# Two layers of a hybrid diffusion backbone: the low parts of the differential keys in 128-row tiles with a zero half, and a rotary step in place

## The chip, the core and the metric

The kernel runs on one core of a Trainium2 chip. The core has a matrix engine (TensorE, PE in the rows; its loads of the stationary operand are shown apart as PEld), VectorE (DVE), ScalarE (ACT), GpSimd (POOL) and SyncE (SP), each with its own queue of instructions that it works off in order, and 16 DMA engines. The metric is the device time of one launch in microseconds (us); less is better.

## What is computed

Two layers work on 640 tokens: 128 context tokens (block 0) and 512 latent tokens (blocks 1 to 4). Each layer has three parallel mixers, a gated merge and a feed-forward part. The change touches one of the mixers, the differential attention. It has 4 heads; each has two queries and two keys of 64 channels, and one value of 128:

```python
def _diff_attention(q, k, v, lam, lam_init):
    s = jnp.einsum('bqhcd,bkhcd->bhcqk', q, k).astype(jnp.float32) * DIFF_HD ** -0.5
    p = jax.nn.softmax(s, axis=-1)
    a = p[:, :, 0] - lam * p[:, :, 1]
    o = jnp.einsum('bhqk,bkhe->bqhe', a.astype(v.dtype), v)
    return (_head_rmsnorm(o) * (1.0 - lam_init)).astype(v.dtype)
```

Latent queries see 640 keys (128 cached ones and the 512 latent ones), context queries see the 128 context keys. Queries and keys of latent tokens are rotated first (`_rope`): x becomes x cos + x' sin, where x' is x with its two halves of 32 channels exchanged and one of them negated.

## The kernel before

All matrix products are made of float32r parts: a value is a high part that the format holds, and the rest as a low part, and a product is the sum of high by high, high by low and low by high. Time is spent mostly in such triples of products (lines 131 to 133 and 1087 to 1089).

The program is written stage by stage: latent attention (`mla`), differential attention (`diff`), retention (`ret`), merge and output projection, feed-forward part; and this twice. A scheduler then sets the order of the instructions on each engine, from the program's order and its own estimate of when each can start. During the attention stages, pieces of other products (gates of line 995 and 996, values of the retention of lines 786 to 789, all with tile G) are handed out by `fill()` between the steps of the attention, one to three pieces a step, so that the matrix engine has work while the softmax runs.

In `diff` each head is built by `build(hd)`, one head ahead of its use: GpSimd issues the DMAs that fetch values (tile V), keys (rk) and queries (rq); `rope` (lines 417 to 429) rotates them with four VectorE operations and two scratch tiles; ScalarE and VectorE make high and low parts; transposes on TensorE (lines 729, 730, 748) bring channels to the partitions, and copies put the result into K1, K2 and Q. For half c of a head (c is 0 or 1), K1 holds in its 128 rows the high part of key c twice. K2 holds the low parts of both: rows 0 to 63 for c = 0, rows 64 to 127 for c = 1. Q holds in 128 rows the high and the low part of query c, the high part where K2 has its rows. So one score takes two products into the same bank, one over 128 rows and one over 64:

```python
pe.matmul(o, Q[:, c, q0:q0 + 128], K1[:, c, k0:k0 + n], start=True, stop=False)
pe.matmul(o, Q[rows, c, q0:q0 + 128], K2[rows, k0:k0 + n], start=False, stop=True)
```

These are lines 807 and 808, with `rows = slice(64 * c, 64 * c + 64)`. For a latent block they come four times (two halves c, two groups of 320 keys), for the context block twice, with 128 keys. Two tiles S of two banks each take the scores in turn.

`diff_head` then runs, for each block in the order 1, 2, 3, 4, 0: the row maximum on VectorE (line 435), the exponential on ScalarE (line 437, into tile dp, four buffers), the weighted difference of the two halves on VectorE (line 821, into tile aw, one buffer), five transposes of aw (line 833), a copy on ScalarE (tile at, two buffers), and five products with V (line 837). The second half, from the transposes on (`diff_av`), is issued one block later than the first. After the last block of a head `diff_end` normalises the head and transposes it (line 851); the tile osb that it reads has one buffer, so the first product with V of the next head waits until those transposes are done.

Of the kernel before, what the change touches and what calls it, by code (L numbers as in the profile page):

```python
# [21 lines left out]
P = 128  # L22
# [3 lines left out]
T = 640  # L26
# [9 lines left out]
NA = 416            # columns of the first product of the latent attention; 256 more follow  # L36
FFN_PARTS = ((0, 8), (8, 16), (16, 22))

# columns of the constant table
C_ID, C_ONE, C_DF, C_DB, C_SEL, C_VEC = 0, 128, 256, 384, 512, 514  # L40
C_C64, C_S64, C_C32, C_S32, C_END = 520, 776, 1032, 1160, 1288
# columns of the per-partition parameter table
V_ADA, V_N1, V_N2, V_FG, V_QN, V_KVN, V_END = 0, 96, 112, 128, 136, 142, 146
# columns of the replicated-row table
# [3 lines left out]
class Kern:  # L48
# [25 lines left out]
    def G(self):  # L74
        """A bank for a product: two in turn, one of them only while attention has the other."""
        self.gi ^= 1
        tag = "G" if self.gi or self.filling else "O"
        return self.ps.tile([P, 512], F32, tag=tag, name="G", bufs=1)
# [11 lines left out]
    def plan(self, points, *gens):  # L90
        """Spread the pieces of (generator, number of pieces[, from, to]) evenly over the next calls of fill()."""
# [25 lines left out]
    def load_w(self, src, cols):  # L117
        """A weight unit [128, cols] from DRAM, as a part that float32r holds and the rest."""
# [8 lines left out]
    def mm3(self, out, steps):  # L127
        """out = sum of lhsT^T rhs over steps of (lhs_hi, lhs_lo, rhs_hi, rhs_lo)."""
# [6 lines left out]
    def rsqrt(self, out, ssq, n, mul, mul2=1.0):  # L135
        """out = mul2 / sqrt(ssq * mul + EPS), for [128, n]."""
# [19 lines left out]
    def setup(self):  # L156
# [12 lines left out]
        # silu of the two conditioning vectors, padded to 32 columns  # L169
# [7 lines left out]
    def rows_setup(self):  # L177
        # log_sigmoid(x) = min(x, 0) - log1p(exp(-|x|)), log1p(e) = 2 atanh(e / (2 + e))
# [38 lines left out]
    def ada_vectors(self, pool):  # L217
        """silu of the two conditioning vectors on every partition."""
# [8 lines left out]
    def ada_rows(self, l, b0, b1, pool):  # L227
        """Modulation with output columns on partitions and the sums on VectorE, a column block a step."""
# [16 lines left out]
    def mod_scale(self, l, which):  # L245
        """A = norm_g * (1 + sc) as [128, 8, 2]; which 0 for the mixers, 1 for the ffn."""
# [10 lines left out]
    def square(self, h, k, x, pool):  # L257
        """Adds the squares of row tile k of a half of x to its sum."""
# [26 lines left out]
    def modulate(self, l, which, h, k, xn, a, ht, pool):  # L285
        """Row tile k of h = xn * A + sh, in float32r parts."""
# [13 lines left out]
    def norm(self, l, which, h, x, a, pool, ps):  # L300
        """h-th half of rmsnorm(x) * A + sh from the sum of squares, in float32r parts (hi, lo) [128, 8, n]."""
# [9 lines left out]
    def start(self):  # L311
        """First norm and first part of the first product, as the columns of the modulation come in."""
# [79 lines left out]
    def tok(self, act, k, b):  # L392
        """(hi, lo) stationary block b of an activation in two halves."""
        h, o = (0, 128 * b) if b < 2 else (1, 128 * b - 256)
        hi, lo = act[h]
        return hi[:, k, o:o + 128], lo[:, k, o:o + 128]

    def a_steps(self, act, b, units):
        """For 128 tokens of block b, act^T W; units: list of (hi, lo, first k, n k) with [128, nk, N]."""
# [17 lines left out]
    def rope(self, pool, out, x, b, nb, nh, hd, tag="avs"):  # L417
        """out = rope(x) for sample blocks b .. b + nb: x [128, nb, nh, hd]."""
# [13 lines left out]
    def softmax(self, sv, p, z, scale, tot=None):  # L432
        """p = exp(scale (sv - max sv)), tot = sum p, z = 1 / tot, for one score row a partition in sv."""
# [7 lines left out]
    def mla(self, l, act, yraw, pool, first=None):  # L441
# [10 lines left out]
        # the k tiles hold two heads each time: rows 0:64 k_nope, rows 64:96 k_pe  # L452
        NK = 3
        kts = [pool.tile([P, 2, TK], F32R, name=f"kt{i}") for i in range(NK)]
        for g in range(2):
# [12 lines left out]
            if g == 0:  # L468
                self.rsqrt(rs[:, 0, :], ss[:, 0, :], NB, 1.0 / 256)
                # decoupled keys  # L470
# [15 lines left out]
                # compressed keys and values  # L486
# [43 lines left out]
        # decoupled queries of all heads, by tokens  # L530
# [81 lines left out]
    def mla_av(self, pool, v, hh, blks, pt, n, y, last=None):  # L612
        """y [64, n] += p^T v over key blocks; pt(kb) gives (hi, lo) [128, n]."""
# [11 lines left out]
    def mla_head(self, pool, qt, q0, kt, v, hh, y, last=None):  # L625
        """Two blocks of sample queries of one head."""
# [55 lines left out]
    def diff(self, l, act, yhi, ylo, ctx):  # L682
# [4 lines left out]
        # lambda  # L687
# [9 lines left out]
        K1, K2, Q, V = {}, {}, {}, {}  # L697
        a6 = "p (a c r) -> p a c r"

        def build(hd):  # L700
# [8 lines left out]
            # keys  # L709
            k1 = K1[hd] = pool.tile([P, 2, TK], F32R, tag="K1", name="K1", bufs=2)  # L710
            k2 = K2[hd] = pool.tile([P, TK], F32R, tag="K2", name="K2", bufs=2)
# [6 lines left out]
            self.rope(pool, rv[:, 2:6], rv[:, 2:6], 0, 4, 2, 64, tag="rp")  # L718
            for j in range(3):
# [13 lines left out]
                d.tensor_copy(k2[:, cs], t2[:, 0:256])  # L733
            # queries, as hi(q1) lo(q1) lo(q2) hi(q2)
# [4 lines left out]
            self.rope(pool, rv[:, 1:5], rv[:, 1:5], 0, 4, 2, 64, tag="rp")  # L739
# [19 lines left out]
    def diff_proj(self, l, act, pool):  # L759
        """Queries, keys, values of the differential attention, by tokens, to DRAM; a generator."""  # L760
# [15 lines left out]
    def ret_values(self, l, act, pool):  # L776
        """Values and doubled silu gates of the retention, by tokens, to DRAM; a generator."""
# [15 lines left out]
    def diff_head(self, pool, Q, K1, K2, V, nlam, lam_init, yhi, ylo):  # L793
# [3 lines left out]
        for b in (1, 2, 3, 4, 0):  # L797
# [4 lines left out]
            for c in range(2):  # L802
                S = self.S()
                rows = slice(64 * c, 64 * c + 64)
                for j in range(2 if b else 1):
                    o, k0, n = (S[:, j, 0:320], 128 + 320 * j, 320) if b else (S[:, 0, 0:128], 0, 128)
                    pe.matmul(o, Q[:, c, q0:q0 + 128], K1[:, c, k0:k0 + n], start=True, stop=False)  # L807
                    pe.matmul(o, Q[rows, c, q0:q0 + 128], K2[rows, k0:k0 + n], start=False, stop=True)  # L808
# [8 lines left out]
            # p0 / t0 - lam p1 / t1 = (p0 - (lam t0 / t1) p1) / t0, the last division after the product with v  # L817
            r = zt[:, 4:5]
            d.scalar_tensor_tensor(r, zs[1][0], nlam, zs[0][1], op0=ALU.mult, op1=ALU.mult)
            aw = pool.tile([P, T], F32, tag="aw", name="aw", bufs=1)  # L820
# [354 lines left out]
    def run(self):  # L1175
# [95 lines left out]
        xctx.close()  # L1271


# [1 line left out]
def consts():  # L1275
    f = np.float32
    i = np.arange(128)
# [117 lines left out]
```

## Time and profile before

| | |
|---|---|
| median of 3 timed runs | 2520.76 us (2518.72 to 2521.29) |
| span of the profiled execution | 2522.9 us |
| TensorE busy in the span | 2471.6 us (98%) |
| VectorE, ScalarE, GpSimd busy | 1500.7, 987.9, 170.8 us |
| differential attention, layer 0 and layer 1 | about 297 to 500 us, and 1535 to 1740 us |

The profiled execution's span is the only time that it has; it is 2.1 us (0.08%) longer than the median of the timed runs. Products on TensorE overlap: the duration that a row gives is that of one product from its start to its modelled end, and the next one may start long before that. What a product costs the engine is therefore read from the distance between two starts in the timeline, not from its duration.

### The profile page before, as it was taken

Reading aid. Unit: us, or ns where it says so; the run is one execution under the profiler, and the core shown is the slowest. Engines: PE = TensorE matmul, PEld = TensorE weight load, DVE = VectorE, ACT = ScalarE, POOL = GpSimd, SP = SyncE. Lnnn points to the kernel's source line nnn. Section 1 sums busy time; section 2 is a strip of 40 time slices with the busy share of each in tenths; the row PEclk is TensorE's granted clock in tenths of the full one; section 3 lists DMA queues with packets and bytes.
Section 4 is the critical chain, followed back from the end, with each engine's and each line's share of the span. In section 5 each row is a group of like instructions: output and inputs, shape, how many; then the busy total and the mean of one; then the engine's idle time right before and its main releaser. Section 6 shows DMA issues by size and latency. Waiting matters only on the chain.

```text
span 2522.9 us, 42747 instructions
## 1 busy us (share of the span) xinstructions
PE 2471.6 (98%) x17236; PEld 2378.8 (94%) x17236; DVE 1500.7 (59%) x3439; ACT 987.9 (39%) x2102; POOL 170.8 (7%) x298
## 2 busy tenths in 40 slices
PE   8999999999999999999999999999999999999997
PEld 5999988899999999999999998889999999999997
DVE  5877665466798676585477866655663562323334
ACT  5656454532324322222376654554222352122123
POOL 0000210010010000010000012001000000000001
PEclk9999999999999999999999999999999999999999
DMA  6212321131553454453231123113222221222221
GB/s 259 76 56 70 101 65 52 64 132 59 186 182 126 142 164 157 139 184 107 65 126 60 52 76 115 62 44 114 79 96 88 72 71 67 84 68 84 67 74 61
DMA packets 70677, 248.94 MB, mean 99 GB/s; under 512 B 9840, under 2 KB 10064, under 8 KB 69584
## 3 DMA queue, kind: packets, MB, share of 16 engines
q1 hardware_dynamic: 46944, 164.12, 19.6%
q0 software_dynamic: 23248, 81.36, 9.8%
q8 instruction: 135, 2.21, 0.4%
q10 hardware_dynamic: 288, 0.73, 0.1%
q14 instruction: 62, 0.51, 0.1%
HBM read 225.97 MB, written 20.22 MB: 98 GB/s over the span
## 4 chain that ended last, share of the span: by engine, by line
PE 91%; issue 3%; DVE 3%; ACT 2%; DMA 1%; POOL 0%; DVEq 0%; ACTq 0%; POOLq 0%
PE G L131 13%; PE G L132 12%; PE G L133 12%; PE S L1089 8%; PE S L1088 8%; PE S L1087 8%; PE S L131 6%; PE S L132 6%; PE S L133 6%; PE S L808 2%; PE S L807 1%; PE Tp L645 1%; PE O L837 1%; PE O L620 1%; PE O L619 1%
## 5 line engine op out<-in xcount | busy, mean ns | idle before, releaser
L112 ACT CAST whi<-raw 128x1024 fp32r<-128x1024 f32 (+4 forms) x298 | 299.2, 1018 | 755.6 <-PE G L132 265.4
L115 DVE TENSOR_TENSOR wlo<-raw,whi 128x1024 fp32r<-128x1024 f32 (+4 forms) x298 | 349.1, 1182 | 358.4 <-ACT whi L112 356.2
L131 PE MATMUL G<-ghi,whi 128*128 128x256 f32 (+1 forms) x704 | 217.2, 309 | 3.1 <-DVE x L1049 3.1
L133 PE MATMUL G<-ghi,wlo 128*128 128x384 f32 (+1 forms) x704 | 216.5, 308 | 0.0
L132 PE MATMUL G<-glo,whi 128*128 128x384 f32 (+1 forms) x704 | 216.4, 308 | 0.0
L1087 PE MATMUL S<-h1hi,whi 128*128 128x384 f32 x640 | 214.0, 334 | 0.0
L1088 PE MATMUL S<-h1lo,whi 128*128 128x384 f32 x640 | 213.9, 334 | 0.0
L1089 PE MATMUL S<-h1hi,wlo 128*128 128x384 f32 x640 | 213.9, 334 | 0.0
L1089 PE MATMUL S<-h0hi,wlo 128*128 128x256 f32 x704 | 199.2, 283 | 1.0 <-DVE wlo L115 0.9
L1088 PE MATMUL S<-h0lo,whi 128*128 128x256 f32 x704 | 198.8, 283 | 0.0
L1087 PE MATMUL S<-h0hi,whi 128*128 128x256 f32 x704 | 198.1, 283 | 0.0
L238 DVE SCALAR_TENSOR_TENSOR junk<-rawr,csr 128x1024 bf16<-128x1024 f32 x160 | 194.9, 1218 | 1.3
L131 PE MATMUL G<-whi,h1hi 128*128 128x256 f32 x624 | 179.3, 288 | 2.7 <-ACT rvs L786 1.0
L133 PE MATMUL G<-whi,h1lo 128*128 128x256 f32 x624 | 177.9, 285 | 0.0
L132 PE MATMUL G<-wlo,h1hi 128*128 128x256 f32 x624 | 177.1, 284 | 0.0
L1049 DVE SCALAR_TENSOR_TENSOR x<-G,mod,x 128x128 f32<-128x128 f32 (+1 forms) x192 | 77.4, 435 | 138.1 <-PE G L133 137.6
L435 DVE TENSOR_REDUCE mx<-S 128x1 f32<-128x640 f32 (+1 forms) x160 | 113.8, 714 | 75.1 <-PE S L808 53.6
L1089 PEld LDWEIGHTS S<-h0hi,wlo 128*128 128x128 f32 x704 | 134.6, 191 | 2.8 <-DVE wlo L115 2.5
L131 PEld LDWEIGHTS G<-ghi,whi 128*128 128x128 f32 x704 | 132.1, 188 | 4.6 <-DVE x L1049 3.3
L1088 PEld LDWEIGHTS S<-h0lo,whi 128*128 128x128 f32 x704 | 134.3, 191 | 0.3
L1087 PEld LDWEIGHTS S<-h0hi,whi 128*128 128x128 f32 x704 | 134.3, 191 | 0.0
L132 PEld LDWEIGHTS G<-glo,whi 128*128 128x128 f32 x704 | 132.1, 188 | 0.2
(428 smaller groups left out, 6908.0 us busy)
## 6 DMA issues: line engine op xcount, KB each, us to landing
raw<-w_ffn_in SPq DMA_DIRECT2D x88, 512.0 KB, 3.6
rawr<-w_adat POOLq DMA_DIRECT2D x80, 512.0 KB, 3.9
raw<-w_gate SPq DMA_DIRECT2D x48, 512.0 KB, 3.3
raw<-w_ffn_out SPq DMA_DIRECT2D x32, 512.0 KB, 3.7
raw<-w_diff SPq DMA_DIRECT2D x24, 512.0 KB, 3.4
raw<-w_branch SPq DMA_DIRECT2D x24, 512.0 KB, 3.7
raw<-w_ret SPq DMA_DIRECT2D x24, 512.0 KB, 3.3
raw<-w_ada SPq DMA_DIRECT2D x16, 512.0 KB, 9.7
```

The source lines that it names most:

```text
L112: (eng or self.act).copy(hi, src)
L115: (eng or self.dve).tensor_tensor(lo, src, hi.bitcast(F32), op=ALU.subtract)
L131: self.pe.matmul(out, lh, rh, start=i == 0, stop=False)
L132: self.pe.matmul(out, lh, rl, start=False, stop=False)
L133: self.pe.matmul(out, ll, rh, start=False, stop=i == n - 1)
L238: self.tc.keep_in_program_order(d.scalar_tensor_tensor(junk, raw, 1.0, self.csr[:, i, :], op0=ALU.mult, op1=ALU.mult, accum_out=mod[:, n, ...
L435: self.dve.tensor_reduce(mx, sv, axis=AX.XY if len(sv.shape) == 3 else AX.X, op=ALU.max)
L808: pe.matmul(o, Q[rows, c, q0:q0 + 128], K2[rows, k0:k0 + n], start=False, stop=True)
L1049: self.dve.scalar_tensor_tensor(x[h][:, n, c0:c1], ps[:, c0:c1], g[:, n, gi:gi + 1], x[h][:, n, c0:c1], op0=ALU.mult, op1=ALU.add)
L1087: self.pe.matmul(o, lh, rh, start=k == 0, stop=False)
L1088: self.pe.matmul(o, lh, rl, start=False, stop=False)
L1089: self.pe.matmul(o, ll, rh, start=False, stop=k == nk - 1)
```

## The change

There are four edits, all in `diff` and what it calls.

1. K2 is no longer one tile with both halves. There are two tiles `K2z`, made once per layer (one for even and one for odd heads), each of 128 rows by 2 halves by 768 keys. For c = 0 rows 64 to 127 are set to zero on GpSimd, for c = 1 rows 0 to 63. The copy of the low parts (line 733 before) becomes two copies of 64 rows each. The second product of a score now takes all 128 rows of Q and of K2z; the zero rows add nothing.
2. `rope_in_place` takes the place of `rope` for the keys and queries of this stage. It has the same four operations, in another order, with one scratch tile of one buffer.
3. `aw` is no tile of its own: the weighted difference overwrites the first of the two tiles dp.
4. Tile `at` has one buffer instead of two.

Comments are removed throughout the file; they are left out here.

```diff
+    def rope_in_place(self, pool, x, b, nb, nh, hd, tag):
...
+        u = pool.tile([P, nb * nh * hd], F32, tag=tag, name="rp", bufs=1).rearrange("p (a h d) -> p a h d", a=nb, h=nh)
+        d = self.dve
+        d.tensor_tensor(u[:, :, :, 0:hh], x[:, :, :, hh:hd], s[:, :, :, 0:hh].to_broadcast([P, nb, nh, hh]), op=ALU.mult)
+        d.tensor_tensor(u[:, :, :, hh:hd], x[:, :, :, 0:hh], s[:, :, :, hh:hd].to_broadcast([P, nb, nh, hh]), op=ALU.mult)
+        d.tensor_tensor(x, x, c, op=ALU.mult)
+        d.tensor_tensor(x, x, u, op=ALU.add)
...
+        k2z = [pool.tile([P, 2, TK], F32R, name=f"K2z{i}") for i in range(2)]
+        for t in k2z:
+            nc.gpsimd.memset(t[64:128, 0, :].bitcast(F32), 0.0)
+            nc.gpsimd.memset(t[0:64, 1, :].bitcast(F32), 0.0)
...
-            k2 = K2[hd] = pool.tile([P, TK], F32R, tag="K2", name="K2", bufs=2)
+            k2 = K2[hd] = k2z[hd % 2]
...
-            self.rope(pool, rv[:, 2:6], rv[:, 2:6], 0, 4, 2, 64, tag="rp")
+            self.rope_in_place(pool, rv[:, 2:6], 0, 4, 2, 64, "rp")
...
-                d.tensor_copy(k2[:, cs], t2[:, 0:256])
+                d.tensor_copy(k2[0:64, 0, cs], t2[0:64, 0:256])
+                d.tensor_copy(k2[64:128, 1, cs], t2[64:128, 0:256])
...
-                rows = slice(64 * c, 64 * c + 64)
...
-                    pe.matmul(o, Q[rows, c, q0:q0 + 128], K2[rows, k0:k0 + n], start=False, stop=True)
+                    pe.matmul(o, Q[:, c, q0:q0 + 128], K2[:, c, k0:k0 + n], start=False, stop=True)
...
-            aw = pool.tile([P, T], F32, tag="aw", name="aw", bufs=1)
+            aw = ps[0]
...
-            at = pool.tile([P, T], F32, tag="at", name="at", bufs=2)
+            at = pool.tile([P, T], F32, tag="at", name="at", bufs=1)
```

The scheduler gives the two stages of `diff` a new order; outside of them the order of every engine stays, and that of SyncE, which issues the weight loads, is the same throughout. The stage holds the same matrix products as before. Three places show what moves. The names with K stand for K1 and K2 of one head, G for a bank that a filled-in product takes, Tp for a bank of transposes.

On TensorE, the scores of the first latent block of the first head in layer 0, first before:

```order
L807 MATMUL S<-K_3873,Q 128x320
L808 MATMUL S<-K_3874,Q 128x320
L729 MATMUL Tp<-identr,kh 128x128 x4
L807 MATMUL S<-K_3873,Q 128x320
L808 MATMUL S<-K_3874,Q 128x320
L807 MATMUL S<-K_3873,Q 128x320
L808 MATMUL S<-K_3874,Q 128x320
L807 MATMUL S<-K_3873,Q 128x320
L808 MATMUL S<-K_3874,Q 128x320
```

and after:

```order
L825 MATMUL S<-K_3879,Q 128x320
L826 MATMUL S<-K2z_3868,Q 128x320
L825 MATMUL S<-K_3879,Q 128x320
L826 MATMUL S<-K2z_3868,Q 128x320
L825 MATMUL S<-K_3879,Q 128x320
L826 MATMUL S<-K2z_3868,Q 128x320
L825 MATMUL S<-K_3879,Q 128x320
L826 MATMUL S<-K2z_3868,Q 128x320
L767 MATMUL Tp<-identr,qs 128x128 x4
L747 MATMUL Tp<-identr,kh 128x128 x4
```

The eight products of the block stay eight and stay in pairs; the transposes that stood among them now stand behind them.

On GpSimd, the start of the stage in layer 0 (V, rk and rq are values, keys and queries that come in by DMA), first before:

```order
L152 DMA ra<-rows 128x256
L704 DMA V<-cdv 128x128
L706 DMA V<-dproj 128x128
L707 DMA V<-dproj 128x4x128
L704 DMA V<-cdv 128x128
L706 DMA V<-dproj 128x128
L707 DMA V<-dproj 128x4x128
L713 DMA rk<-dproj 128x128
```

and after:

```order
L152 DMA ra<-rows 128x256
L714 MEMSET K2z_3868 64x768
L715 MEMSET K2z_3868 64x768
L714 MEMSET K2z_3869 64x768
L715 MEMSET K2z_3869 64x768
L722 DMA V<-cdv 128x128
L724 DMA V<-dproj 128x128
L725 DMA V<-dproj 128x4x128
L722 DMA V<-cdv 128x128
L724 DMA V<-dproj 128x128
L725 DMA V<-dproj 128x4x128
L731 DMA rk<-dproj 128x128
```

The four fills of zeros stand ahead of all fetches of the first two heads.

On VectorE, the key and query parts of the first head in layer 0 (rp is the scratch tile of the rotation, kl and qs hold low parts), first before:

```order
L426 TENSOR_TENSOR rp<-rq,ct 128x512
L427 TENSOR_TENSOR rp<-rq,ct 128x8x32
L428 TENSOR_TENSOR rp<-rq,ct 128x8x32
L733 COPY K_3874<-Tp 128x256
L115 TENSOR_TENSOR kl<-rk,kh 128x256 x2
L429 TENSOR_TENSOR rq<-rp 128x512
L115 TENSOR_TENSOR qs<-rq,qs 128x128
```

and after:

```order
L439 TENSOR_TENSOR rp<-rq,ct 128x8x32
L751 COPY K2z_3868<-Tp 64x256
L752 COPY K2z_3868<-Tp 64x256
L440 TENSOR_TENSOR rp<-rq,ct 128x8x32
L115 TENSOR_TENSOR kl<-rk,kh 128x256 x2
L441 TENSOR_TENSOR rq<-rq,ct 128x512
L115 TENSOR_TENSOR wlo<-raw,whi 128x1024
L442 TENSOR_TENSOR rq<-rq,rp 128x512
```

One copy of the low key part has become two, and the operation over 512 columns of the rotation comes after the two over halves.

## Rows read from the trace of the kernel before

**Rows 1.** Page, part 4: the chain that ended last, by engine.

```profile
PE 91%; issue 3%; DVE 3%; ACT 2%; DMA 1%; POOL 0%; DVEq 0%; ACTq 0%; POOLq 0%
```

**Rows 2.** Lines 807 and 808: duration ns min/median/max, first and last start, forms.

```profile
L807 PE MATMUL S<-K,Q x144: 220/410/417, 316.3 to 1724.2; 128*128 128x320 f32 x128, 128*128 128x128 f32 x16
...
L808 PE MATMUL S<-K,Q x144: 322/410/413, 316.5 to 1724.5; 64*128 64x320 f32 x128, 64*128 64x128 f32 x16
```

**Rows 3.** Timeline of PE, one latent block: start us, duration us, instruction.

```profile
346.81 0.39 PE L807 MATMUL S<-K,Q 128*128 128x320 f32 x1
...
349.51 0.45 PE L131 MATMUL G<-h1hi,whi 128*128 128x384 f32 x1
349.79 0.34 PE L132 MATMUL G<-h1lo,whi 128*128 128x384 f32 x1
349.97 0.33 PE L133 MATMUL G<-h1hi,wlo 128*128 128x384 f32 x1
```

**Rows 4.** Timeline of PEld in the same block; in brackets idle time before.

```profile
347.47 0.19 PEld L807 LDWEIGHTS S<-K,Q 128*128 128x128 f32 x1 [0.15 <-issue]
347.81 0.18 PEld L808 LDWEIGHTS S<-K,Q 64*128 64x128 f32 x1 [0.16 <-issue]
```

**Rows 5.** Timeline of PE, scores of the latent attention (96 rows, 320 columns).

```profile
137.07 0.31 PE L131 MATMUL S<-kt,qt 96*128 96x320 f32 x1
...
137.95 0.31 PE L131 MATMUL S<-kt,qt 96*128 96x320 f32 x1
```

**Rows 6.** Timeline of PEld, the load for the product at 137.07.

```profile
136.93 0.19 PEld L131 LDWEIGHTS S<-kt,qt 96*128 96x128 f32 x1
```

**Rows 7.** Timeline of PE, half a context block (128 columns) of the differential attention.

```profile
354.76 0.22 PE L807 MATMUL S<-K,Q 128*128 128x128 f32 x1
354.91 0.33 PE L808 MATMUL S<-K,Q 64*128 64x128 f32 x1
...
355.44 0.33 PE L131 MATMUL G<-h1hi,whi 128*128 128x384 f32 x1
```

**Rows 8.** Timeline of PE, scores of the latent attention with 128 columns.

```profile
147.76 0.27 PE L132 MATMUL S<-kt,qt 96*128 96x128 f32 x1
147.87 0.27 PE L133 MATMUL S<-kt,qt 96*128 96x128 f32 x1
```

**Rows 9.** Busy time by stretch: us, PE, PEld, DVE, ACT, POOL busy, PEclk, DMA share, GB/s.

```profile
300.00:380.00 80.00, 79.02 (x508) 68.84 (x506) 55.52 (x140) 45.53 (x118) 11.62 (x19) 1.00 0.24 78
...
100.00:140.00 40.00, 39.90 (x317) 39.63 (x317) 30.82 (x73) 23.71 (x55) 3.24 (x6) 1.00 0.23 77
```

**Rows 10.** Waits of DVE, 297 to 500 us: total us, times, longest us.

```profile
DVE mx L435 <- PE S L808: 26.9, 27, 2.2
DVE aw L821 <- PE Tp L833: 13.7, 9, 4.1
```

**Rows 11.** Line 733, columns as in rows 2.

```profile
L733 DVE CAST K<-Tp x24: 411/420/426, 302.9 to 1666.2; 128x256 fp32r<-128x256 f32 x24
```

**Rows 12.** Line 808 from 300 to 380 us, columns as in rows 2.

```profile
L808 PE MATMUL S<-K,Q x30: 323/410/413, 316.5 to 375.8; 64*128 64x320 f32 x28, 64*128 64x128 f32 x2
```

**Rows 13.** Timeline of POOL at the start of the stage in layer 0.

```profile
279.58 0.75 POOL L707 DMA_DIRECT2D V<-dproj  x1
288.45 0.54 POOL L713 DMA_DIRECT2D rk<-dproj  x1 [8.11 <-DVE lpr L690]
```

**Rows 14.** Groups of POOL by line and form: busy us, mean ns, then idle before.

```profile
L1169 POOL TENSOR_TENSOR x<-x,nr 128x384 f32<-128x384 f32 x4 | 4.8, 1234 | 619.0 <-ACT nr L278 619.0
...
L1370 POOL MEMSET const-float32-0.0<- 128x1 f32 x1 | 0.1, 98 | 0.2 <-issue 0.2
```

**Rows 15.** Busy time in a stretch of lower clock, columns as in rows 9.

```profile
429.70:433.10 3.40, 3.40 (x17) 3.40 (x17) 2.46 (x14) 0.58 (x1) 0.00 (x0) 0.50 0.02 5
```

**Rows 16.** Timeline of PE, from the last product with V of head 0 to its end.

```profile
367.94 0.49 PE L837 MATMUL O<-V,at 128*128 128x128 f32 x2
...
386.97 0.76 PE L851 MATMUL Tp<-ct,osb 128*128 128x128 f32 x5
```

More of the change, by code (lines that the diff above doesn't have):

```diff
@@ L429, in rope @@
         d.tensor_tensor(out, t, u, op=ALU.add)
+    def rope_in_place(self, pool, x, b, nb, nh, hd, tag):
+        cc, ss = (C_C64, C_S64) if hd == 64 else (C_C32, C_S32)
+        hh = hd // 2
+        c = self.ct[:, cc + hd * b:cc + hd * (b + nb)].rearrange("p (a d) -> p a d", a=nb).unsqueeze(2).to_broadcast([P, nb, nh, hd])
+        s = self.ct[:, ss + hd * b:ss + hd * (b + nb)].rearrange("p (a d) -> p a d", a=nb).unsqueeze(2)
+        u = pool.tile([P, nb * nh * hd], F32, tag=tag, name="rp", bufs=1).rearrange("p (a h d) -> p a h d", a=nb, h=nh)
[4 more added lines that the diff above has]
+        d.tensor_tensor(x, x, u, op=ALU.add)
     def softmax(self, sv, p, z, scale, tot=None):
@@ L738, in build @@
             rv = r.rearrange("p a (c d) -> p a c d", c=2)
-            self.rope(pool, rv[:, 1:5], rv[:, 1:5], 0, 4, 2, 64, tag="rp")
+            self.rope_in_place(pool, rv[:, 1:5], 0, 4, 2, 64, "rp")
             for b0, nb in ((0, 1), (1, 2), (3, 2)):
```

## The prediction

> **What bounds the kernel now.** I began with the chain of work that ended last: 91% of it is TensorE, and 3% is "issue", time in which an engine stood still although nothing that the profile shows held it [rows 1]. So what shortens TensorE's own work counts nearly in full, as long as nothing else takes its place, and the "issue" share asks for a look of its own. The lines that the change touches come next: 144 products each on lines 807 and 808, of which 128 have 320 columns and 16 have 128, the first over 128 rows, the second over 64 [rows 2].
>
> Their durations say little, since products overlap. The timeline says more. In one latent block the first of eight score products starts at 346.81, the product after them at 349.51 and the next at 349.79, where that kind then goes on at 0.17 to 0.18 us a piece [rows 3]. Eight products in 2.70 us are 0.34 each. The weight loads show where that goes: the load for line 807 starts at 347.47 and the one for line 808 at 347.81, each after 0.15 to 0.16 us in which the load path did nothing [rows 4]. Nothing is loaded ahead.
>
> The reader should hold the scores of the latent attention beside this. They have as many columns and 96 rows, one shape after another, and start every 0.147 us (137.07 to 137.95, six products) [rows 5]; the load for the product at 137.07 begins at 136.93, under the product ahead of it [rows 6]. The same work thus goes at 0.147 where the row shape stays, and at 0.34 where 128 and 64 rows alternate. That the alternation is the cause, and not something else in these pairs, is my reading of the two rows; the change takes away the alternation and nothing else of it.
>
> **The change part by part.** *Second product over 128 rows.* In the block above, first product to the second one after the scores is 2.98 us [rows 3]. At the other pace it would be 8 x 0.147 for the scores and 0.17 for the product at 349.51, 1.35 us. The loss is 1.63. A little of it may stay: transposes stand ahead of the first score, and the first gap may be long for that reason too. I take 0.09 for it, half of what a gap between two shapes costs over one shape (0.34 - 0.147 = 0.19). So 1.54 to 1.63 a block, and with 32 latent blocks (4 blocks, 4 heads, 2 layers) 49 to 52 us. For the context block one pair and its follower take from 354.76 to 355.44, 0.68 us [rows 7], where 128 columns with one shape go at 0.11 [rows 8]: 0.11 + 0.11 + 0.17 = 0.39, so 0.29 lost, and 16 such pairs give 4.6. Together 54 to 57 us. Where a block is cut by other products each cut costs part of a gap, which the new order merely moves. I take 54.
>
> The Trainium skill has a rule that speaks against this term. Its page "TensorE: Matmul & The Clock Gate" (Part 3, The mechanism) says that a weight load overlaps a running product "only when row_grp differs", that is, only when the two use different rows of the array. By that rule products over all rows would keep their loads exposed, the sum of this term would be 0, and the time would stay near 2521. The trace disagrees [rows 5, 6]: products over the same 96 rows have their loads hidden.
>
> *Two copies for one.* Line 733's copy of 128 rows takes 0.42 us, 24 times [rows 11]. I price a 64-row copy of as many columns between half and all of that and take all, since the number of columns is unchanged: 24 more at 0.42 are 10.1 us of VectorE in both layers. VectorE is busy 55.5 of 80 us in the densest stretch [rows 9], and 26.9 us of its idle time in one layer is waiting for scores [rows 10]. That idle time covers it: nothing on the path. If the cover is gone, the price is the 10.1.
>
> *Rotation in place.* The same four operations over the same columns on one engine: nothing. With one scratch buffer the next rotation waits for the last, and both are on VectorE, in order.
>
> *aw inside dp.* VectorE no longer waits for the transposes of the block before to free aw; that is 13.7 us of its waits in layer 0, the longest 4.1 [rows 10]. Behind that wait the maxima of the next block and splits of weights were queued. TensorE was fed meanwhile, so I count no gain; it is slack that the next edit may use. In return one of four dp buffers stays taken until its transposes, and an exponential may wait for it.
>
> *One buffer for at.* ScalarE's copy now waits for the last product with V of the block before. Where only a few products stand between two such groups TensorE could wait. That goes into the allowance below.
>
> *Zeros.* Four fills per layer stand on GpSimd ahead of the fetches of V, keys and queries. This trace has no such fill. From below: a fill of one column takes 0.098 us, so 0.4 for four. From above: an operation with two inputs over 384 columns takes 1.234 [rows 14], so 768 columns 2.5, and 9.9 for four. I lean to the upper half, since the columns count. The first fetch of keys waited 8.11 us on GpSimd anyway, for VectorE [rows 13], so it is late by at most 1.8 us, and the first score comes some 28 us after that fetch (288.45 to 316.3) [rows 2, 13]. I take nothing; 0 to 3.6 in both layers is in the range.
>
> *Less slack.* With TensorE ahead by 1.6 us a block, the softmax has less time. In the densest stretch TensorE is not busy for 0.98 of 80 us [rows 9]. Over the two stages, some 400 us, that is 4.9. I allow as much again. VectorE reaches 77% (30.82 of 40) in the latent attention with TensorE idle for 0.10 us [rows 9], so a high share alone doesn't starve it.
>
> *The clock.* For 3.4 us in this stage the granted clock was 0.50, which is 1.2 in place of 2.4 GHz [rows 15], and 17 products started where twice as many could. If it fell because the pairs had left TensorE thinly used, and doesn't fall any more, about 1.7 us a layer come back, 3.4 in all. I count that in the range only.
>
> The sum: 54 saved, 4.9 given back, 49 net. Against the profiled span of 2522.9 us that is 2474; the timed runs had a median 2.1 lower, so 2472.
>
> **The rivals.** *VectorE becomes the bound.* From 300 to 380 us stand 30 pairs, 28 of them long [rows 12], which shortens the stretch by 28 x 0.386 + 2 x 0.29 = 11.4 to 68.6 us (0.386 is twice 0.34 less 0.147). VectorE would have 55.5 us and some 9 more copies (three heads of three), 59.3, or 86%. If it can't be fed above the 77% that the latent attention shows, the stretch takes 77 us, 8.4 more; in two layers 16.8. The time is then 2520.8 - 54 + 16.8 = 2484. For it: the chain maximum, exponential, difference runs across engines that work in order. Against it: 77% was reached while TensorE set the pace, so it is no ceiling.
>
> *It doesn't do what it says.* The pairs keep 0.34 us, because the loads stay exposed for another reason (both products of a pair load the same part of Q and add to one bank). Then only the costs are left: 2521, or 2531 with all 10.1 us of copies on the path. By the page's rule above this would be the outcome. Rows 5 and 6 speak against it.
>
> *Slower, at the heads' ends.* The next head's products with V wait until the last head is normalised and transposed. From the last product with V of head 0 to these transposes pass 19.0 us [rows 16], which TensorE fills with other products. The in-place difference keeps dp buffers taken in just that time. If the next head's exponentials then starve TensorE, up to 19 us are bare at each of six such places, 114 in all: 2520.8 - 54 + 114 = 2581. It decides from 9 us a place (6 x 9 = 54). Against it: in the new order 136 products and transposes stand between those two points, 112 before.
>
> **How the numbers follow.** The forecast has 0.70, VectorE as the bound 0.19, no effect 0.07 (split between no change and slower), the heads' ends 0.04, of which half would end slower. The forecast's own range is 2460 (57 saved, 3.4 from the clock, no stall) to 2478. The range of eight in ten reaches to the VectorE rival with a little more, 2486. About 0.2% (5 us) is what a measurement of this kernel tells from no change: faster by more 0.92, within it 0.04, slower 0.04.
>
> **What would show it.** In the profile after: score products in one latent block start every 0.15 us, their loads begin under the product ahead, and the "issue" share falls. The second products read 128 rows with durations near 0.31 us. The copies of low parts number 48, at 0.3 to 0.42 us. The two stages are each some 25 us shorter and everything outside of them is as long as before. The prediction is wrong in its main term if the starts stay 0.34 apart, and wrong in its allowance if TensorE waits for line 435, 437 or the difference of line 821 for more than some 5 us a layer.

## The result, and the profile after

The changed kernel takes 2488.05 us (median of 4 runs, 2486.88 to 2489.07), the kernel before in the same comparison 2521.03 (2518.72 to 2523.84). The ratio is 0.9868, with a 95% interval of 0.9854 to 0.9882. The profiled execution spans 2485.8 us, 37.1 less than before. So the change gains 33 us where 49 were forecast, and the time lies 2 us above 2486, the top of the range of eight in ten. Spans show 4 us more gain than that, since the profiled execution of the kernel before was a long one: a span is some 1.9 us shorter than the time of the same execution (2485.8 against 2487.65 for the changed kernel), so its 2522.9 stands for a time of some 2525, an estimate.

The gain is there where it was expected. Part 4 of the page, the chain that ended last by engine, answers to [rows 1]; "issue" fell from 3% to 2%:

```profile
PE 91%; DVE 4%; issue 2%; ACT 2%; DMA 1%; POOL 0%; DVEq 0%; ACTq 0%; POOLq 0%
```

The two score lines are now 825 and 826. Their durations, with the columns of [rows 2]:

```profile
L825 PE MATMUL S<-K,Q x144: 221/309/415, 316.1 to 1688.4; 128*128 128x320 f32 x128, 128*128 128x128 f32 x16
L826 PE MATMUL S<-K2z,Q x144: 273/309/323, 316.3 to 1688.5; 128*128 128x320 f32 x128, 128*128 128x128 f32 x16
```

The same latent block as in [rows 3], on the timeline of PE (start us, duration us):

```profile
340.59 0.31 PE L826 MATMUL S<-K2z,Q 128*128 128x320 f32 x1
340.74 0.31 PE L825 MATMUL S<-K,Q 128*128 128x320 f32 x1
...
341.47 0.31 PE L826 MATMUL S<-K2z,Q 128*128 128x320 f32 x1
341.62 0.38 PE L855 MATMUL O<-V,at 128*128 128x128 f32 x2
```

And the loads, which answer to [rows 4]:

```profile
340.59 0.19 PEld L825 LDWEIGHTS S<-K,Q 128*128 128x128 f32 x1
340.74 0.19 PEld L826 LDWEIGHTS S<-K2z,Q 128*128 128x128 f32 x1
```

Starts are 0.147 us apart in place of 0.34, and each load begins when the product ahead of it begins. No bracket with idle time is left.

What took part of the gain back stands among the waits of PE from 290 to 510 us (total us, times, longest us):

```profile
PE G L131 <- DVE rvs L808: 5.7, 3, 4.2
PE G L131 <- ACT gt L1013: 1.5, 4, 0.6
PE S L825 <- ACT dp L450: 1.0, 2, 0.7
PE Tp L869 <- DVE osb L864: 0.6, 1, 0.6
PE O L855 <- ACT at L852: 0.5, 1, 0.5
```

Before, the list of the same stage (290 to 530 us) has four lines and 3.2 us in all: 1.5 for gt, 0.7 and 0.5 for rvs, 0.5 for osb, none longer than 0.5. After, it is 11.1 us with five smaller lines that are left out here, and half of it is waiting for VectorE's work on pieces of the retention values (`rvs`), 4.2 us of it in one wait at the end of the stage. Layer 1 shows 6.0 us for the same line. The chain that ended last tells what it hangs on (start us, us, what):

```profile
485.97 0.12 PE G L132
...
489.75 0.41 POOL rS L903
490.27 0.91 POOL rV L905
491.18 0.88 POOL rSG L906
492.06 0.87 POOL rV L905
492.93 8.16 DMA rproj<-rvs
501.11 0.39 ACT rvs L807
501.53 0.43 DVE rvs L808
502.00 0.42 PE G L131
502.42 0.21 PE G L132
```

The retention values leave by way of two staging tiles: ScalarE fills one, and GpSimd issues its write-back to DRAM (`rproj`). Here four loads for the next stage (rS, rV, rSG, rV, of which the last three carry 640 KB each) are issued ahead of a write-back. It starts at 492.93 and lands 8.16 us later. ScalarE can't fill that tile again until then, and TensorE stands still. The last load ahead of it, issued at 492.06, took 8.7 us, so the write-back lands some 0.3 us after that load. Its data had been ready since 489.5, when VectorE was done with them. In the kernel before, the two loads of values go out while no write-back is due, and the next write-back takes 3.4 us to land:

```profile
505.33 1.80 POOL L887 DMA_DIRECT2D rV<-rproj  x2
510.35 0.60 POOL L790 DMA_DIRECT2D rproj<-rvs  x1 [3.22 <-DVE Dm L867]
```

The row of the write-back's issue on GpSimd (at 492.93) is only 0.57 us long, so this is not seen in GpSimd's busy time. The Trainium skill says so: "Perfetto Trace Analysis", section "Per-instruction lifecycle: what the profiler-reported window actually captures", puts a DMA's data movement outside of the reported window. The trace agrees (0.57 against 8.16 us).

The stall has a second price. Busy time by stretch, with PEclk third from the end (columns as in [rows 9]), at the end of the stage in either layer:

```profile
502.10:505.50 3.40, 3.40 (x17) 3.40 (x18) 0.22 (x1) 0.00 (x0) 1.07 (x2) 0.52 0.58 207
1724.10:1727.50 3.40, 3.40 (x18) 3.40 (x18) 0.00 (x0) 0.00 (x0) 0.91 (x2) 0.51 0.53 202
```

The granted clock falls to the lower level (1.2 GHz) right after the wait, and on the chain above products take 0.21 us where they took 0.12. The fall of [rows 15] is gone, and these have come.

### The profile page after: what moved, and what is told of

The parts are those of the page before. It is cut to its first block, busy times and chain, and to the rows that moved or that the text cites. A ratio compares the mean times of both kernels' runs of the same rounds, so it can differ in the third digit from the quotient of the medians.

```text
span 2485.8 us, 42801 instructions
## 1 busy us (share of the span) xinstructions
PE 2419.1 (97%) x17236; PEld 2367.1 (95%) x17236; DVE 1511.3 (61%) x3463; ACT 992.8 (40%) x2102; POOL 177.0 (7%) x306
## 4 chain that ended last, share of the span: by engine, by line
PE 91%; DVE 4%; issue 2%; ACT 2%; DMA 1%; POOL 0%; DVEq 0%; ACTq 0%; POOLq 0%
PE G L131 13%; PE G L132 12%; PE G L133 12%; PE S L1107 8%; PE S L1106 8%; PE S L1105 8%; PE S L131 6%; PE S L132 6%; PE S L133 6%; PE O L855 1%; PE Tp L658 1%; PE S L825 1%; PE O L633 1%; PE O L632 1%; PE S L826 1%
## 5 line engine op out<-in xcount | busy, mean ns | idle before, releaser
L131 PE MATMUL G<-whi,h0hi 128*128 128x256 f32 x416 | 121.6, 293 | 12.0 <-DVE rvs L808 11.7
```

The costliest lines, as they stand in the source:

```text
L131: self.pe.matmul(out, lh, rh, start=i == 0, stop=False)
```

## The experiments

Ratios are against runs of the kernel before on the same chip in the same comparison, with 95% intervals; 0.1% is 2.5 us. In all kernels with the third staging buffer the diff is that of the first of them.

### Is it the row shape? Second product over 64 rows again, in the changed kernel

```diff
-                    pe.matmul(o, Q[:, c, q0:q0 + 128], K2[:, c, k0:k0 + n], start=False, stop=True)
+                    rows = slice(64 * c, 64 * c + 64)
+                    pe.matmul(o, Q[rows, c, q0:q0 + 128], K2[rows, c, k0:k0 + n], start=False, stop=True)
```

> The changed kernel, with its second score product over the 64 rows that hold the low part, as before; tiles, zeros, copies and the other three edits stay. Theory A (alternating row shapes cost some 53 us; the missing 12 us went to the end of the stage, where VectorE's and ScalarE's work on the retention values waits for write-backs): the starts go back to 0.34 us, the wait of TensorE for the retention values stays near 5 us a layer, and the time is 2488 + 53 = 2541, or 5 less if the small waits of the softmax go. Theory B (the denser stage lacks VectorE time, and that took the gain): with the stage slack again nothing is lost, 2521 to 2525. Theory C (copies and zeros cost it): some 2531 with no wait at the stage's end.

Measured: 2537.83 us, ratio 1.0069 (1.0054 to 1.0084). The starts are 0.34 us apart again, and the wait for the retention values stays, at 5.1 us in layer 0. Against the 0.9868 of the changed kernel that is 0.0201 of 2521, or 51 us for the row shape alone. Without it, the rest of the change makes the kernel 17 us slower than before.

### Is it the change of shape, or the 64 rows? The kernel before, products grouped by shape

```diff
                     pe.matmul(o, Q[:, c, q0:q0 + 128], K1[:, c, k0:k0 + n], start=True, stop=False)
+                for j in range(2 if b else 1):
+                    o, k0, n = (S[:, j, 0:320], 128 + 320 * j, 320) if b else (S[:, 0, 0:128], 0, 128)
                     pe.matmul(o, Q[rows, c, q0:q0 + 128], K2[rows, k0:k0 + n], start=False, stop=True)
```

> The kernel before with the four products of a half of a score block in another order: both over 128 rows, then both over 64. Shape changes in a latent block fall from eight to four, all else stays. If the change of shape is what costs (0.193 us each): 4 x 32 fewer changes x 0.193 = 25 us, 2496. If a product over 64 rows costs by itself, or a load onto the rows in use: 2521. Loads under a product of the same shape, exposed at a change.

Measured: 2496.34 us, ratio 0.9902 (0.9887 to 0.9917), 25 us faster than before, and the edit is the order of the products alone. On the timeline of PE (x2 are two products in a row):

```profile
343.74 0.54 PE L807 MATMUL S<-K,Q 128*128 128x320 f32 x2
344.21 0.56 PE L810 MATMUL S<-K,Q 64*128 64x320 f32 x2
344.70 0.56 PE L807 MATMUL S<-K,Q 128*128 128x320 f32 x2
345.19 0.56 PE L810 MATMUL S<-K,Q 64*128 64x320 f32 x2
```

Two products now take 0.47 to 0.49 us, as much as one step of 0.34 and one of 0.147 together. (The single starts do not split that way: they lie 0.23 to 0.25 us apart, within a pair as at a change.) Two products over 64 rows take no longer than two over 128, so the 64 rows as such are not slow; a change of shape adds 0.19 us to the sum. The Trainium skill, "TensorEngine Tiling (Array Packing)", section "Tiling Modes", has the rule that bears on it: changing the tiling mode, not just the tile, drains the engine. The trace agrees, with 0.19 us a change.

### What do edits 2 to 4 cost alone? The kernel before with them, K2 as it was

```diff
-            self.rope(pool, rv[:, 2:6], rv[:, 2:6], 0, 4, 2, 64, tag="rp")
+            self.rope_in_place(pool, rv[:, 2:6], 0, 4, 2, 64, "rp")
...
-            aw = pool.tile([P, T], F32, tag="aw", name="aw", bufs=1)
+            aw = ps[0]
...
-            at = pool.tile([P, T], F32, tag="at", name="at", bufs=2)
+            at = pool.tile([P, T], F32, tag="at", name="at", bufs=1)
```

> The kernel before with edits 2 to 4 alone (rotation in place, weighted difference inside dp, one buffer for at); K2 and its products as before. Theory A, with the cause in these edits (they change which memory comes free when, and with it GpSimd's order of loads and write-backs at the stage's end): TensorE waits some 5 us a layer for the retention values at the end of the stage, 2521 + 10 to 13 = 2531 to 2534. Theory B (density) and theory C (copies and zeros): 2521, no such wait.

Measured: 2540.74 us, ratio 1.0075 (1.0058 to 1.0092): 19 us slower, more than theory A gave. TensorE waits for the retention values, as in the changed kernel, over both layers:

```profile
PE G L131 <- DVE rvs L800: 11.9, 6, 4.6
```

The 64-row kernel above has the copies and zeros too and is no slower than this one, so no cost of copies and zeros shows, though the two kernels also differ in the tiles that hold the low key parts. Theory C falls; theory B falls too, since here the stage is not denser than before. The profiled execution, 17.4 us longer than that of the kernel before, shows where the time is: TensorE's waits in the two stages are 21.7 us (9.1 before), and ahead of the last fall of the clock at the kernel's end the lower level is granted for 27 us in all (14 before). As products start half as often at that level, this is an estimate of 7 us beside the 12.6 of waits, which together cover it.

### Taking the wait away in three ways

A third staging buffer:

```diff
-                r = pool.tile([P, 384], F32, tag="gt", name="rvs", bufs=2)
+                r = pool.tile([P, 256], F32, tag="rvs", name="rvs", bufs=1) if (NB * j + b) % 3 == 2 else pool.tile([P, 384], F32, tag="gt", name="rvs", bufs=2)
```

> The changed kernel with a third staging buffer for the retention values (every third piece gets a tile of its own). Theory A, with the ring as the limit: the waits of TensorE for these values fall from 11.7 us to under 4, the stretch of half clock behind them goes too, 2474 to 2480. If it is the late landing of the write-backs, and one more buffer only moves the wait by a piece: 2481 to 2486. Theories B and C: 2488.

Measured: 2479.3 us, ratio 0.9835 (0.9820 to 0.9850). The waits over both layers fall from 11.7 to 2.9 us:

```profile
PE G L131 <- DVE rvs L808: 2.9, 4, 1.1
```

and the clock stays up after the stage; ahead of the kernel's end it falls only at 282 us, where it also fell before the change (rows by stretch as above):

```profile
281.00:286.00 5.00, 3.66 (x14) 3.40 (x15) 3.52 (x6) 2.96 (x6) 2.44 (x4) 0.66 0.59 160
502.00:506.00 4.00, 3.54 (x31) 3.34 (x30) 1.09 (x3) 1.13 (x3) 0.54 (x1) 1.00 0.83 271
```

Write-backs issued by ScalarE:

```diff
-                self.pool.dma_start(out=self.rproj[j][:, b, :], in_=r[:, :256])
+                self.act.dma_start(out=self.rproj[j][:, b, :], in_=r[:, :256])
```

> The changed kernel with the write-backs of the retention values issued by ScalarE instead of GpSimd, so they no longer stand behind GpSimd's loads; two staging buffers as in the changed kernel. If the wait at the stage's end comes from the loads ahead of the write-backs: it falls under 2 us a layer, 2476 to 2481. If two buffers are too few in any case: the wait stays near 5 us a layer, 2486 to 2490. If ScalarE's own waiting for VectorE delays copies and exponentials: above 2490.

Measured: 2479.77 us, ratio 0.9835 (0.9820 to 0.9849). The chain of this kernel at the same place:

```profile
488.83 6.19 DMA rproj<-rvs
495.10 0.39 ACT rvs L807
495.52 0.43 DVE rvs L808
```

The write-back starts 4.1 us earlier and lands 6.1 us earlier, yet still takes 6.19 us. The loads moved too. GpSimd no longer stops for the pieces' write-backs, and issues the last load ahead of this one at 487.17 in place of 492.06 (timeline of POOL); that load takes 7.6 us:

```profile
487.17 0.89 POOL L905 DMA_DIRECT2D rV<-rproj  x1
```

So here too the write-back lands 0.3 us after the last load ahead of it. The time is as expected, but the wait is not under 2 us a layer: it is 5.7 us over both layers. That the write-back itself is issued sooner is thus not shown to be what helped; that the loads are out of its way sooner fits the rows as well. The Trainium skill, "DMA: Bandwidth & Descriptors", section "Issuing engines are not separate DMA queues", bears on it: DMAs of all engines share the same 16 DMA engines, and issuing from another saves only the time to issue. The trace agrees: from ScalarE the write-back still takes 6.19 us, behind the loads.

Retention values handed out earlier, so that fewer pieces come after the last head:

```diff
-            self.plan(23, (self.gates(l, 2, act, m, mp), 16, 0.0, 0.7), (self.ret_values(l, act, mp), 20, 0.6, 0.95))
+            self.plan(23, (self.gates(l, 2, act, m, mp), 16, 0.0, 0.7), (self.ret_values(l, act, mp), 20, 0.6, 0.86))
```

> The changed kernel with the retention values handed out a little earlier (0.60 to 0.86 of the plan instead of 0.60 to 0.95), so that two write-backs instead of four stand behind GpSimd's loads and fewer pieces come after the last head. If pieces and loads that crowd at the stage's end are the cause: the wait halves or goes, 2477 to 2484. If it only moves into the attention: 2488.

Measured: 2480.56 us, ratio 0.9837 (0.9822 to 0.9851).

Two cures at once, first the earlier pieces with the third buffer:

> The kernel of a_span with the third staging buffer too. If both ease the same wait: 2475 to 2480, no further than the third buffer alone (2479). If what is left elsewhere in the stage's end matters too: 2470 to 2475.

Measured: 2480.91 us, ratio 0.9840 (0.9824 to 0.9857). Then ScalarE's write-backs with the earlier pieces:

> The changed kernel with the write-backs issued by ScalarE and the retention values handed out earlier. If both ease the same wait: 2476 to 2481, as each alone. If the last waits for retention values (2.7 to 3.0 us a layer with ScalarE's write-backs, 1.9 with the earlier pieces) go too: 2472 to 2476.

Measured: 2479.67 us, ratio 0.9834 (0.9819 to 0.9848). Five kernels end at 2479 to 2481, some 8 us below the changed kernel. They ease one and the same thing, and what is left lies elsewhere.

### Which of the edits? Each alone, in the kernel before

The edits are the parts of the diff of edits 2 to 4 above. Edit 4, one buffer for at:

> The kernel before with edit 4 alone: one buffer for at. In the order of GpSimd at the stage's end, a load of gates (rSG) and one of values (rV) now stand ahead of the last two write-backs; with edits 2 to 4 three loads stood ahead of four. Theory A (this edit turns that order and so makes TensorE wait at the end of the stage): a wait of some 3 to 6 us a layer for the retention values and the clock behind it, 2519 + 6 to 16 = 2525 to 2535. If edit 2 or 3, or only all three together, make it: 2519 to 2521.

Measured: 2533.64 us, ratio 1.0052 (1.0037 to 1.0067); TensorE waits for the retention values for 2.7 us in layer 0, less than the 3 to 6 expected, and for tile at 1.1. Its waits in the two stages come to 18.0 us, 9 more than before. Edit 3, the difference inside dp:

> The kernel before with edit 3 alone: the weighted difference inside dp. GpSimd's order stays that of before. Theory A: no wait at the stage's end, 2519, or up to 3 less since VectorE no longer waits for the transposes. If the held dp buffers are what cost the 21 us of edits 2 to 4: 2525 to 2540, with TensorE waiting for line 437's exponentials.

Measured: 2529.35 us, ratio 1.0037 (1.0025 to 1.0049), with the wait for retention values at 0.7 us in layer 0, as before, and TensorE waiting for dp for 0.3 us. Neither reading that I had set down fits. The profiled execution is 5.3 us longer than that of the kernel before: TensorE's waits in the two stages are 12.1 us (9.1 before), with tile at foremost (2.2 us over both layers), and the clock falls for 3.4 us five times ahead of the kernel's end, once more than before, which is an estimate of 1.7 us. The rest of the 9 us is open. These kernels have another order of the scheduler each, so a price here is that of the edit with the order that comes of it. Edits 2 to 4 with the third buffer:

> The kernel before with edits 2 to 4, and the third staging buffer. Of the 22 us that edits 2 to 4 cost alone, the buffer gives back what belongs to the stage's end: waits 11 and clock some 4 to 7, so 2524 to 2530. If their cost is elsewhere (held dp buffers, one at buffer): 2536 to 2541.

Measured: 2530.65 us, ratio 1.0036 (1.0023 to 1.0049). The buffer gives back 10 us of the 19, as it does 8 in the changed kernel. Edit 2, the rotation in place:

> The kernel before with edit 2 alone: rotation in place, one scratch buffer. If the cost beyond the stage's end is in edits 3 and 4: 2518 to 2522, no change. If it is in the single scratch buffer: 2525 or more.

Measured: 2540.64 us, ratio 1.0080 (1.0065 to 1.0095). The edit that seemed the most harmless costs 20 us alone, as much as all three; their costs don't add. One of the waits of POOL from 500 to 525 us, and what stands on the chain there:

```profile
POOL rS L895 <- PE Tp L862: 5.9, 1, 5.9
```

```profile
509.54 0.56 PE Tp L862 x5
...
510.38 0.46 POOL rS L895
...
510.97 0.53 POOL rS L896
511.50 0.30 POOL rV L898
...
512.40 0.46 POOL rV L898
...
513.28 7.85 DMA rproj<-rvs
521.21 0.39 ACT rvs L799
521.63 0.43 DVE rvs L800
```

The load of the retention states (rS) waits 5.9 us for the transposes that read osb, at the very end of the last head. The loads of values and the write-backs are queued behind it, and the write-back at 513.28 lands at 521.13. TensorE then waits 5.8 us. To tell whether the operations or the smaller scratch do it, the same kernel with two scratch buffers:

```diff
-        u = pool.tile([P, nb * nh * hd], F32, tag=tag, name="rp", bufs=1).rearrange("p (a h d) -> p a h d", a=nb, h=nh)
+        u = pool.tile([P, nb * nh * hd], F32, tag=tag, name="rp", bufs=2).rearrange("p (a h d) -> p a h d", a=nb, h=nh)
```

> The kernel before with the in-place rotation, but with two scratch buffers, so that the scratch takes as much memory as before. If the smaller scratch is the cause, by the place in memory that rS then takes over: rS no longer waits for the transposes of osb, no wait of TensorE for the retention values above 2 us a layer, 2518 to 2523. If the in-place operations or their order are the cause: 2535 to 2542 as in b_rope.

Measured: 2524.41 us (10 runs), ratio 1.0013 (1.0004 to 1.0023), just above the expected 2523. The load of rS goes out at 503.33 and waits for nothing, ahead of osb's transposes:

```profile
503.33 0.56 POOL L895 DMA_DIRECT2D rS<-st  x1
503.88 0.53 POOL L896 DMA_DIRECT2D rS<-st  x1
504.39 1.80 POOL L898 DMA_DIRECT2D rV<-rproj  x2
```

So the size of the scratch does it, not the operations; what is left, 3 us, is just clear of noise. That works by way of memory, as I read it: the tiles of the retention stage take over the memory that the differential stage gives back, and 2 KB less of scratch puts rS where osb was. The rows show the wait for osb's reader, not the addresses.

### Undoing edits 3 and 4 in the changed kernel

The transposed weights in the second dp tile, which gives at two buffers in effect:

```diff
-            self.later(lambda *x, b=b, w=w, nk=nk, kb0=kb0, aw=aw, z0=zs[0][0]: self.diff_av(pool, b, nk, kb0, aw, z0, V, osb, ssq))
+            self.later(lambda *x, b=b, w=w, nk=nk, kb0=kb0, aw=aw, at=ps[1], z0=zs[0][0]: self.diff_av(pool, b, nk, kb0, aw, z0, V, osb, ssq, at))
...
-            at = pool.tile([P, T], F32, tag="at", name="at", bufs=1)
```

> The changed kernel without a tile at: the transposed weights go into the second dp tile of the block, which is free by then, so there are in effect two buffers again. Two write-backs, not four, stand behind the loads on GpSimd. If edit 4 is the cause of the stage's end: the wait there halves or goes and the small waits for at go, 2474 to 2483. If it is only the staging ring: 2486 to 2488. If held dp buffers starve the softmax: above 2488.

Measured: 2484.0 us, ratio 0.9859 (0.9844 to 0.9874), just above the range expected and 4 us below the changed kernel, with intervals that overlap. With the third staging buffer too:

> The kernel of a_atp with the third staging buffer too. Theory A: what is left of the wait at the stage's end goes, 2472 to 2478, at or below a_ring3 (2479). If held dp buffers starve the softmax: above a_ring3 by as much as a_atp is above the changed kernel.

Measured: 2483.09 us, ratio 0.9851 (0.9835 to 0.9868). That isn't below the third buffer alone. Room for real tiles had to be made first, from the kernel with the earlier pieces:

```diff
-            self.rope_in_place(pool, rv[:, 2:6], 0, 4, 2, 64, "rp")
+            for i in (0, 2):
+                self.rope_in_place(pool, rv[:, 2 + i:4 + i], i, 2, 2, 64, "rp")
...
-                kl = pool.tile([P, 2, 2, 64], F32R, tag="kl", name="kl", bufs=2)
+                kl = pool.tile([P, 2, 2, 64], F32R, tag="kl", name="kl", bufs=1)
```

> The kernel of a_span (retention values handed out earlier) with 2 KB a partition freed: the rotation in two halves of two blocks with a scratch tile of half the size (eight operations on VectorE instead of four), and one buffer for kl. It is the base for the next two. If VectorE has time to spare: within 3 us of a_span, 2477 to 2484. If VectorE or the kl buffer binds: above 2485.

Measured: 2480.63 us, ratio 0.9842 (0.9827 to 0.9857). On that, two buffers for at:

> a_room_span with edit 4 undone (two buffers for at). If edit 4 makes the rest of the cost: 3 to 8 us below a_room_span, 2471 to 2478, and the waits for at and osb in TensorE's list go. If edit 3 does: as a_room_span.

Measured: 2487.84 us, ratio 0.9872 (0.9855 to 0.9888). And aw as a tile of its own:

> a_room_span with edit 3 undone (aw a tile of its own). If the held dp buffers make the rest of the cost: 3 to 8 us below a_room_span, 2471 to 2478, and TensorE no longer waits for the exponentials of tile dp. If edit 4 does: as a_room_span.

Measured: 2483.4 us, ratio 0.9851 (0.9836 to 0.9865). Giving the buffers back gains nothing, and the kernel with the second at buffer is 7 us slower. That is not the price of a buffer: TensorE waits there for at 1.9 us and for dp 2.7, against 0.2 and 0.7 with one buffer, so the scheduler's new order came out worse. My reading that the held buffers are what the changed kernel lacks finds no support.

## Why the prediction was off, step by step

**Where it ends.** The gain is all in the two stages. The first and last start of the retention stage's transposes, before and after (columns as in [rows 2]), move by 18.9 us after one layer and by 36.2 after both, of 37.1 in the span; some 25 a layer were forecast:

```profile
L902 PE MATMUL Tp<-ct,rr x40: 271/272/273, 528.2 to 1805.6; 128*128 128x128 f32 x40
```

```profile
L920 PE MATMUL Tp<-ct,rr x40: 271/272/273, 509.3 to 1769.4; 128*128 128x128 f32 x40
```

**Second product over 128 rows.** Right, in mechanism and nearly in size: 54 us were taken, undoing it costs 51. All else in the change costs 17 us, where 4.9 were counted; that is where the forecast broke. The reading of the two rows, alternation and not the rows as such, is shown by the grouped kernel (25 us expected, 25 measured). The rule of the Trainium skill that spoke against it ("TensorE: Matmul & The Clock Gate", Part 3, The mechanism: a load overlaps a product only when the row groups differ) would have left 2521 or more; the trace disagrees, loads onto the same 128 rows begin under the product ahead (340.59 and 340.74 above).

**Copies and zeros.** Right. The copies measure 0.41 and 0.43 us (48 of them) and are hidden. The zeros are cheaper than I leaned to, 2.9 us for four (the last of them below), and the first fetch of keys goes out at 286.62, earlier than in [rows 13]:

```profile
278.77 0.73 POOL L715 MEMSET K2z<- 64x768 f32 x1
...
286.62 0.54 POOL L731 DMA_DIRECT2D rk<-dproj  x1 [3.06 <-DVE lpr L703]
```

**Rotation in place, and aw and at: this step failed.** I priced edit 2 at nothing and looked for the cost of edits 3 and 4 among the work inside the attention. Together they cost 19 us alone, and of that some 10 us sit at the end of the stage, in GpSimd's queue, which I had read only at the start of the stage: the loads for the next stage stand ahead of write-backs there. In the changed kernel, the cures give back 8 us. Which edit sets that order of loads and write-backs in the changed kernel is not shown: edits 2 to 4 bring such a wait in the kernel before, edit 2 alone does too, but by another way (a load that waits for osb), and the larger tiles of edit 1 may move memory as well.

**Less slack.** The allowance was 4.9 us for waits among the softmax; TensorE's waits in the stage grew by 7.9 us in layer 0 (11.1 less 3.2), and by 15 over both layers. Of that 5.0 a layer (5.7 less 0.7 in layer 0) is the retention values, which the term did not hold; the other 5 in all are close to its size. So the allowance was right for what it named, and the sum lacked a term of 10 us for the end of the stage. The bound that was to show the allowance wrong, more than 5 us a layer for the softmax, was not reached (1.0 us for dp).

**The clock.** Falls at the places of the stage did go, and one at its end came in each layer. Ahead of the kernel's end the profile has three falls of 3.4 us in place of four, so an estimate of 1.7 of the 3.4 us came back.

**VectorE as the bound.** Its time (2484) was the closest, its mechanism not there. From 300 to 380 us VectorE is busy 67.45 us, 84%, past the 77% at which the rival saw a ceiling, with TensorE at 77.88:

```profile
300.00:380.00 80.00, 77.88 (x570) 76.32 (x569) 67.45 (x172) 51.34 (x128) 12.05 (x19) 1.00 0.28 89
```

**The heads' ends, and no effect.** Neither came; at the first, TensorE waits 0.6 us for osb.

Even cured, the kernel stands 7 to 9 us above the forecast of 2472. Of that 3 us are the main term (51 for 54), and in the kernel with the third buffer some 4 are waits: 18 us in the two stages, 9 more than before, where 4.9 were allowed. What stays open is which edit makes the end of the stage crowd in the changed kernel, and half of the 9 us that edit 3 costs alone.

## What to carry to other kernels

Count changes of row shape on TensorE, not rows: at 0.19 us each, padding with zeros, or merely grouping products by shape, paid here. When an edit changes the size of a tile or the number of its buffers, look at the stage that takes the memory over, at its loads, and at what is queued behind them on the issuing engine, not only at the tile's own users. A staging ring of two that just covers a write-back is a debt that the next edit may call in, and a stall of a few us may cost the clock on top.

## What the hardware showed that I had not expected

A write-back of 128 KB that lands in 2.9 us as a rule (the median of eight from 470 to 520 us) took 8.16 us with some 2 MB of loads issued ahead of it, and 6.19 us when another engine had issued it. Both times it landed 0.3 us after the last load ahead of it, and in the kernel with edit 2 alone 0.8 us after (521.1 against 520.3). And 4.2 us without work for TensorE were followed by 3.4 us at the lower clock.
